# Start of a seven-product MLP kernel: two w1 blocks per load between the first x blocks, half-column products, and 16-bit turns for the later half of x

## The chip, the cores and the metric

The kernel runs on one core of a Trainium2 chip. The metric is the device time of one execution in microseconds (us). All runs told of here are in the fast state: their granted TensorE clock, the mean over an execution, is 0.989 or more of full speed. PE is the TensorE's matmul unit, DVE the VectorE, ACT the ScalarE, POOL the GpSimd, SP the SyncE, which here only issues DMAs.

## The reference

```python
# x[16,256,512], w1[512,4096], w2[2048,512], all float32
h = x @ w1
gate, value = np.split(h, 2, axis=-1)
h = np.maximum(gate, 0) * value
return (h @ w2).astype(np.float32)
```

## The kernel before

The 4096 rows of x are worked off in four stages of 1024 rows. A stage has a first matmul (16 blocks of w1 columns) and a second one (with w2), and the second one of a stage is interleaved with the first blocks of the next stage. Both matmuls are done with seven products in place of eight, on operands in 16 bit. For that, four sums of parts of x (S1 to S4) and four of parts of w1 (T1 to T4) are needed. In stage 0, DVE makes the former once and POOL the latter for two blocks at a time:

```python
def sums_of(o, eng=nc.vector):                     # L164
    for n, i0, i1, op in (("S1", "A21", "A22", ADD), ("S2", "S1", "A11", SUB), ("S4", "A12", "S2", SUB),
                          ("S3", "A11", "A21", SUB)):
        yield eng.tensor_tensor(o[n], o[i0], o[i1], op=op)

def w1_ops(jb, n, t):                              # L215 to L218, two blocks at a time
    ...
    nc.gpsimd.tensor_tensor(op["T1"], b12, b11, op=SUB)
    nc.gpsimd.tensor_tensor(op["T2"], b22, (op["T1"]), op=SUB)
    nc.gpsimd.tensor_tensor(op["T3"], b22, b12, op=SUB)
    nc.gpsimd.tensor_tensor(op["T4"], b21, (op["T2"]), op=SUB)
```

A block's seven products write three PSUM tiles X, Y, W. ACT copies X into Y after P1, and P6, P7 and P4 add to that copy. `P5` needs S1 and T1, `P3` needs S4, `P7` needs S3, and P4 waits until DVE has read Y for `cc` (L266):

```python
WX = {"P1": ("B11", "A11"), "P2": ("B21", "A12"), "P3": ("B22", "S4"), "P4": ("T4", "A22"),
      "P5": ("T1", "S1"), "P6": ("T2", "S2"), "P7": ("T3", "S3")}
def P1(self):
    ...
    self.mm("P1", self.X, True)
    self.Y = psy.tile([P, TH], F32, name="Y", tag="Y")
    nc.scalar.copy(out=self.Y, in_=self.X)         # L240
```

At the very start, x arrives as eight float32 blocks of 128 rows. PE turns (transposes) each of them into PSUM, and DVE and ACT copy one half each into the 16-bit tiles. Since the sums aren't ready then, the first two blocks of w1 are "plain": eight ordinary products. `keep_busy` puts filler products between the turns:

```python
def turn_first(o, h, b, ps):
    for e in range(4):
        nc.tensor.transpose(ps[:, e * P:(e + 1) * P], xn[h][b][:, e * P:(e + 1) * P], ident)
    for k, copy in ((0, nc.vector.tensor_copy), (1, nc.scalar.copy)):
        copy(out=o[f"A{h + 1}{k + 1}"][:, :, b * P:(b + 1) * P], in_=ps[:, k * 256:k * 256 + 256]...)
...
    turn_first(xo, 0, 2, new_x()); keep_busy(2)        # shortened
    turn_first(xo, 0, 3, new_w()); keep_busy(2)
    plain[0].products(0, *first_half, half)            # the first useful products
    ...
    next(sums)                                         # S1
    plain[0].products(1, *second_half, half)
    next(sums); next(sums)                             # S2, S4
    plain[0].products(1, *second_half, other)
    plain[0].value(); plain[0].gate(1)
    prepare(3)
    plain[1].products(1, *second_half)                 # the last plain products; S3 comes in block 2
```

For the later stages, GpSimd casts x to 16 bit from DRAM to DRAM (a casting load) and SP loads it back with eight transposing loads. DVE's four sums for stage 1 stand, in its order of work, ahead of the two evictions L352 and L357 of stage 0's last output pair.

## Time and profile before

| | before |
|---|---|
| median of three runs (lowest to highest) | 313.85 us (313.25 to 314.24) |
| span of the profiled execution | 311.5 us |
| PE busy | 97% |
| first plain product starts | 8.48 us |
| block 2 (first with seven products) starts | 17.19 us |
| block 4 starts | 23.54 us |

The page's lines of busy time and of the chain of waits that ended last, before:

```profile
PE 302.7 (97%) x1870; PEld 182.8 (59%) x1870; DVE 231.2 (74%) x378; ACT 177.9 (57%) x350; POOL 153.9 (49%) x186
...
PE 69%; ACT 2%; issue 0%
```

PE is the limit. There is little to gain but at the start and in single waits. PE's timeline shows those. A line of a timeline has the start in us, the busy time in us, engine, source line, operation, output and inputs, the shape, the number of instructions, and in brackets how long the engine was idle before and what ended that. PE, before:

```profile
8.26 0.38 PE L150 MATMUL Y<-warm 128*128 128x256 f16 x2
8.48 0.38 PE L288 MATMUL X<-x_A_149,w_B_87 128*128 128x256 f16 x2
...
17.19 0.59 PE L233 MATMUL X<-x_A_149,w_B_87 128*128 128x512 f16 x2
17.62 0.59 PE L233 MATMUL W<-x_S_152,w_T_90 128*128 128x512 f16 x2
18.45 0.59 PE L233 MATMUL X<-x_A_150,w_B_88 128*128 128x512 f16 x2 [0.23 <-ACT Y L240]
...
23.11 0.59 PE L233 MATMUL Y<-x_A_151,w_T_93 128*128 128x512 f16 x2 [0.48 <-DVE cc L266]
23.54 0.59 PE L233 MATMUL X<-x_A_149,w_B_87 128*128 128x512 f16 x2
...
85.27 0.59 PE L233 MATMUL W<-x_S_684,w_T_90 128*128 128x512 f16 x2
86.44 0.60 PE L320 MATMUL Y<-v_T_100,g 128*128 128x256 f16 x4 [0.57 <-DVE o L357]
```

A product of two 512-column matmuls takes 0.43 us from start to start (17.19 to 17.62), one of two 256-column matmuls 0.22. The busy column is longer since successive matmuls overlap, so delays below are counted from start to start: 18.45 − 17.62 − 0.43 = 0.40 us lost for the copy of X into Y. From 8.48 to 17.19 no time is lost. The wait at 86.44 loses 0.74 us (85.27 + 0.43 = 85.70).

DVE and POOL, before, in the same view:

```profile
14.93 0.68 DVE L164 TENSOR_TENSOR x_S_152<-x_S_154,x_A_151 128x1024 f16<-128x1024 f16 x1
15.64 1.65 DVE L164 TENSOR_TENSOR x_S_153<-x_S_152,x_A_149 128x1024 f16<-128x1024 f16 x1
17.33 1.53 DVE L164 TENSOR_TENSOR x_S_155<-x_A_150,x_S_153 128x1024 f16<-128x1024 f16 x1
...
82.98 0.69 DVE L164 TENSOR_TENSOR x_S_684<-x_S_686,x_A_683 128x1024 f16<-128x1024 f16 x1 [2.14 <-DMA x_A_683<-x_598]
...
85.97 0.42 DVE L357 SCALAR_TENSOR_TENSOR o<-Y,pu_1002 128x256 f32<-128x256 f32 x1
```

```profile
15.34 1.40 POOL L215 TENSOR_TENSOR w_T_90<-w_stage 128x512 f16<-128x512 f32 x1 [5.42 <-DMA w_stage<-in_w_dram]
16.82 1.48 POOL L216 TENSOR_TENSOR w_T_91<-w_stage,w_T_90 128x512 f16<-128x512 f32 x1
```

The same sum takes 0.68 us alone (14.93, and 82.98) and 1.65 us beside POOL. S1 begins at 14.93, just before POOL's first subtraction at 15.34, and so is still cheap.

### The profile page before, as it was taken

To read this page: it belongs to the slowest core of one execution; us is meant where nothing else is said; L and a number is where in the kernel's file an instruction comes from. 1 tells how busy PE (TensorE), PEld (TensorE's weight loads), DVE (VectorE), ACT (ScalarE), POOL (GpSimd) and SP (SyncE) were. 2 spreads that over 40 slices of the span, in tenths; PEclk is the share of its full clock that TensorE was granted. 3 is DMA by queue.
4 is the path that set the end of the run, shared out by engine and by line. 5 is a ranking of instruction groups with operands and counts; after the bars stand their busy time and mean duration, and the time that the engine had idled before them with its cause. 6 is when DMAs were issued, how large, how long until landed. Compare 5 with 4: busy or idle time off the path is not lost.

```text
span 311.5 us, 5217 instructions
## 1 busy us (share of the span) xinstructions
PE 302.7 (97%) x1870; PEld 182.8 (59%) x1870; DVE 231.2 (74%) x378; ACT 177.9 (57%) x350; POOL 153.9 (49%) x186
## 2 busy tenths in 40 slices
PE   7999999999999999999999999999999999999993
PEld 3934444588844444478864444458884444448883
DVE  1598888889758888887527888888536888888841
ACT  2688885445855555537675555545776555553230
POOL 2199999920058999400028889700007998700000
PEclk9999999999999999999999999999999999999999
DMA  7978695999784233000355400000335110000132
GB/s 241 354 221 258 183 222 76 202 205 151 214 243 102 70 69 67 2 0 36 136 171 117 117 1 3 0 0 9 128 107 164 37 34 1 0 3 0 69 140 66
DMA packets 37340, 32.87 MB, mean 106 GB/s; under 512 B 14400, under 2 KB 32320, under 8 KB 37184
## 3 DMA queue, kind: packets, MB, share of 16 engines
q1 hardware_dynamic: 31904, 25.70, 27.5%
q0 software_dynamic: 4352, 6.29, 11.8%
q10 hardware_dynamic: 1056, 0.52, 0.6%
q8 instruction: 15, 0.25, 0.3%
q14 instruction: 13, 0.11, 0.1%
HBM read 27.26 MB, written 12.58 MB: 128 GB/s over the span
## 4 chain that ended last, share of the span: by engine, by line
PE 69%; ACT 2%; issue 0%
PE Y L233 20%; PE X L233 13%; PE W L233 13%; PE Y L320 10%; PE X L320 7%; PE W L320 6%; ACT sq L179 1%; ACT Y L240 0%; ACT o L363 0%; ACT pu_1812 L347 0%; PE X L527 0%; ACT pu_2615 L347 0%
## 5 line engine op out<-in xcount | busy, mean ns | idle before, releaser
L170 POOL TENSOR_TENSOR fold<-xh 128x1024 f32<-128x1024 f16 x16 | 30.3, 1895 | 95.0 <-DMA xh<-x_696 35.0
L260 DVE SCALAR_TENSOR_TENSOR cc<-W,pu 128x512 f32<-128x512 f32 x62 | 42.9, 692 | 33.7 <-ACT pu L254 30.5
L254 ACT ACTIVATE pu<-Y 128x512 f32<-128x512 f32 x62 | 37.1, 598 | 34.9 <-PE Y L233 33.7
L240 ACT COPY Y<-X 128x512 f32<-128x512 f32 x62 | 35.4, 571 | 37.3 <-PE X L233 21.2
L173 POOL TENSOR_TENSOR fold<-fold 128x512 f32<-128x512 f32 (+2 forms) x96 | 51.9, 540 | 7.5
L320 PEld LDWEIGHTS <-w_stage 128*128 128x128 f16 x512 | 50.0, 98 | 5.9
L261 DVE SCALAR_TENSOR_TENSOR g<-X,cc 128x512 f16<-128x512 f32 x62 | 42.9, 692 | 2.3
L270 DVE SCALAR_TENSOR_TENSOR g<-Y,cc 128x512 f16<-128x512 f32 x62 | 42.3, 682 | 2.8 <-PE Y L233 2.8
L320 PEld LDWEIGHTS <-g 128*128 128x128 f16 x384 | 37.5, 98 | 9.0 <-issue 0.9
L266 DVE SCALAR_TENSOR_TENSOR cc<-Y,pu 128x512 f32<-128x512 f32 x62 | 42.3, 682 | 0.2
L247 ACT ACTIVATE pu<-W 128x512 f32<-128x512 f32 x62 | 37.1, 599 | 0.0
L164 DVE TENSOR_TENSOR w_stage<-g 128x1024 f16<-128x1024 f16 x32 | 21.4, 686 | 0.2
L233 PEld LDWEIGHTS <-w_T_93 128*128 128x128 f16 x124 | 12.0, 97 | 16.0 <-issue 4.2
L233 PEld LDWEIGHTS <-w_B_88 128*128 128x128 f16 x124 | 12.1, 98 | 15.0 <-issue 1.1
L233 PEld LDWEIGHTS <-w_B_89 128*128 128x128 f16 x124 | 12.1, 98 | 14.8 <-issue 0.3
L233 PEld LDWEIGHTS <-w_T_90 128*128 128x128 f16 x124 | 12.1, 98 | 14.7
L233 PEld LDWEIGHTS <-w_T_91 128*128 128x128 f16 x124 | 12.1, 98 | 14.7
L233 PEld LDWEIGHTS <-w_T_92 128*128 128x128 f16 x124 | 12.1, 98 | 13.8 <-issue 0.2
L233 PEld LDWEIGHTS <-w_B_87 128*128 128x128 f16 x124 | 11.9, 96 | 13.5
L320 PE MATMUL Y<-v_T_100,g 128*128 128x256 f16 x128 | 17.1, 273 | 0.6 <-DVE o L357 0.6
L320 PE MATMUL Y<-v_T_98,w_stage 128*128 128x256 f16 x128 | 16.8, 273 | 0.0
L320 PE MATMUL W<-v_B_96,w_stage 128*128 128x256 f16 x128 | 16.6, 273 | 0.0
(218 smaller groups left out, 565.4 us busy)
## 6 DMA issues: line engine op xcount, KB each, us to landing
out_dram<-o SPq DMA_DIRECT2D x30, 256.0 KB, 2.0
w_stage<-in_w_dram SPq DMA_DIRECT2D x14, 512.0 KB, 5.5
x_598<-in_x_dram POOLq DMA_DIRECT2D x1, 1024.0 KB, 10.1
x_653<-in_x_dram POOLq DMA_DIRECT2D x1, 1024.0 KB, 16.0
x_696<-in_x_dram POOLq DMA_DIRECT2D x1, 1024.0 KB, 19.8
xh<-x_653 SPq DMA_DIRECT2D x4, 256.0 KB, 3.4
xh<-x_598 SPq DMA_DIRECT2D x4, 256.0 KB, 3.9
x_1346<-in_x_dram POOLq DMA_DIRECT2D x1, 1024.0 KB, 7.5
```

Of the source, the lines that this page charges most:

```text
L164: yield eng.tensor_tensor(o[n], o[i0], o[i1], op=op)
L170: nc.gpsimd.tensor_tensor(fold, t, t, op=MULT)
L173: nc.gpsimd.tensor_tensor(fold[:, :, :m], fold[:, :, :m], fold[:, :, m:2 * m], op=ADD)
L233: nc.tensor.matmul(ps, wop[wn][:, b, self.jb * P:(self.jb + 1) * P], self.xo[xn][:, b, :], start=fresh and b == 0, stop=b == 1, skip_group ...
L240: nc.scalar.copy(out=self.Y, in_=self.X)
L247: nc.scalar.activation(self.p5, self.W, COPY, scale=GS)
L254: nc.scalar.activation(self.u2, self.Y, COPY, scale=GS)
L260: nc.vector.scalar_tensor_tensor(out=self.c12, in0=self.W, scalar=GS, in1=self.u2, op0=MULT, op1=ADD)
L261: nc.vector.scalar_tensor_tensor(out=self.g[:, self.jb, :TH], in0=self.X, scalar=0.0, in1=self.c12, op0=MAX, op1=MULT)
L266: nc.vector.scalar_tensor_tensor(out=self.c22, in0=self.Y, scalar=GS, in1=self.p5, op0=MULT, op1=ADD)
L270: nc.vector.scalar_tensor_tensor(out=self.g[:, self.jb, TH:], in0=self.Y, scalar=0.0, in1=self.c22, op0=MAX, op1=MULT)
L320: nc.tensor.matmul(ps, self.op[an][:, i], vop[wn][:, i], start=name in ("P1", "P5") and i == 0, stop=i == NJ // 2 - 1, skip_group_check=True)
```

## The change

The intent is an earlier and denser start. The first two w1 blocks come in one load (rows of 1 KB in place of 512 B), its gate half ahead of x1 and its value half between x1 and x2, so that gate products of half the columns can begin with two x blocks. The later half of x is cast to 16 bit and turned at 16 bit. In the program, the three sums S1, S2, S4 stand ahead of the last plain products, and one last group of plain products moves behind block 2's second product, where it covers the copy of X into Y. The diff, cut to its core:

```diff
-    wl = [(0, 1, 0), (1, 1, 1)] + [(jb, 2, jb % 6) for jb in range(2, NJ, 2)]
+    wl = [(jb, 2, jb % 6) for jb in range(0, NJ, 2)]
 ... (plain_w: DVE and ACT cast these w1 blocks; POOL did most of it before)
-    fetch(0, nc.scalar)
-    fetch_first(0)
-    fetch(1, nc.sync)
+    fetch_first(0, 0)
+    fetch(0, nc.scalar, (0,))
+    fetch_first(0, 1)
+    fetch(0, nc.sync, (1,))
+    fetch_first(0, 2, 3)
+    fetch_first(1, 0, 1, 2, 3)
 ... (turn_first: 16-bit rows and a 16-bit identity for the later half)
+    ys = [new_y(), new_y()]
+    turn_first(xo, 0, 0, *ys)
+    keep_busy(6)
+    turn_first(xo, 0, 1, new_x(), new_x())
+    for y in ys:
+        nc.tensor.matmul(y, warm_b[:, :P], warm_b[:, :TH], start=True, stop=True)
+    for p in plain:
+        p.open()
+        p.part("gate", *first_half, half)
+    turns = new_x()
+    turn_first(xo, 0, 2, turns[:, :2 * P], turns[:, 2 * P:])
+    for p in plain:
+        p.part("value", *first_half, half)
+    turn_first(xo, 0, 3, turns[:, :2 * P], turns[:, 2 * P:])
+    cast_first(0, nc.gpsimd.tensor_copy)
+    cast_first(1, nc.vector.tensor_copy)
+    cast_first(2, nc.gpsimd.tensor_copy)
 ... (16-bit turns between the other plain products, in the banks turns and turns2)
-    next(sums)
-    plain[0].products(1, *second_half, half)
+    plain[1].products(*second_half, half)
     next(sums)
     next(sums)
-    plain[0].products(1, *second_half, other)
+    next(sums)
+    plain[0].products(*second_half, other)
     plain[0].value()
     plain[0].gate(1)
-    plain[1].products(1, *second_half)
+    def last_plain():
+        plain[1].products(*second_half, other)
+        plain[1].value()
+        next(sums)
+        plain[1].gate(1)
 ...
                 if s == 0 and (n, jb) == ("P5", NPLAIN):
-                    next(sums)
-                    plain[1].gate(1)
+                    last_plain()
```

More of the change, by code (lines that the diff above doesn't have):

```diff
@@ L142, in fast_way @@
     ident = wpool.tile([P, P], F32, name="ident")
+    Y = psy.tile([P, TH], F32, name="Y", tag="Y")
     for i in range(NWARM):
-        Y = psy.tile([P, TH], F32, name="Y", tag="Y")
         nc.tensor.matmul(Y, warm_b[:, :P], warm_b[:, :TH], start=True, stop=True)
@@ L201, in load_rows, with load_w1 @@
         return t
-    def load_w1(eng, jb, n, u):
+    def load_w1(eng, jb, n, u, halves=(0, 1)):
         t = w_stage[:, u:u + n].rearrange("p u v -> p (u v)").rearrange("p (g e j) -> p g e j", g=2, e=4)
-        for v in range(2):
+        for v in halves:
             eng.dma_start(out=t[:, v], in_=w1_v[v, :, :, jb * P:(jb + n) * P])
@@ L277, in __init__, with open, part, products @@
             self.g, self.jb = g, jb
-        def products(self, h, a1, a2, cols=(0, TH)):
+        def open(self):
+            self.X = psx.tile([P, TH], F32, name="X", tag="X")
+            self.W = psw.tile([P, TH], F32, name="W", tag="W")
+        def part(self, which, a1, a2, cols):
             js, c = slice(self.jb * P, (self.jb + 1) * P), slice(*cols)
-            if cols[0] == 0:
-                self.X = psx.tile([P, TH], F32, name="X", tag="X")
-                self.W = psw.tile([P, TH], F32, name="W", tag="W")
-            for a, gate, value in ((a1, "B11", "T3"), (a2, "B21", "B22")):
-                for ps, wn in ((self.X, gate), (self.W, value)):
-                    for b in range(2):
-                        nc.tensor.matmul(ps[:, c], wop[wn][:, b, js], a[:, b, c], start=a is a1 and b == 0,
-                                         stop=a is a2 and b == 1)
+            ps, names = (self.X, ("B11", "B21")) if which == "gate" else (self.W, ("T3", "B22"))
+            for a, wn in zip((a1, a2), names):
+                for b in range(2):
+                    nc.tensor.matmul(ps[:, c], wop[wn][:, b, js], a[:, b, c], start=a is a1 and b == 0,
+                                     stop=a is a2 and b == 1)
+        def products(self, a1, a2, cols):
+            if cols[0] == 0:
+                self.open()
+            self.part("gate", a1, a2, cols)
+            self.part("value", a1, a2, cols)
         def value(self):
@@ L389, in advance, with fetch @@
             next(stream, 0)
-    wl = [(0, 1, 0), (1, 1, 1)] + [(jb, 2, jb % 6) for jb in range(2, NJ, 2)]
+    wl = [(jb, 2, jb % 6) for jb in range(0, NJ, 2)]
     ws, copies = {}, []
-    def fetch(i, eng):
+    def fetch(i, eng, halves=(0, 1)):
         if i < len(wl):
@@ L398, in fetch @@
             jb, n, u = wl[i]
-            ws[i] = load_w1(eng, jb, n, u)
+            ws[i] = load_w1(eng, jb, n, u, halves)
     def prepare(i):
@@ L408, in copy_some, with plain_w @@
         del copies[:n]
-    def plain_w(i):
-        jb, n, _ = wl[i]
-        t = ws.pop(i)
+    def plain_w(v):
+        jb, n, _ = wl[0]
         js = slice(jb * P, (jb + n) * P)
-        for n, k, v in (("B11", 0, 0), ("B21", 1, 0), ("T3", 0, 1)):
-            nc.gpsimd.tensor_copy(out=wop[n][:, :, js], in_=t[:, k, :, v])
-        return lambda: nc.scalar.copy(out=wop["B22"][:, :, js], in_=t[:, 1, :, 1])
+        for (wn, k), copy in zip(((("B11", 0), ("B21", 1)), (("T3", 0), ("B22", 1)))[v], (nc.vector.tensor_copy, nc.scalar.copy)):
+            copy(out=wop[wn][:, :, js], in_=ws[0][:, k, :, v])
     def plain_w_end(jb, n, i):
@@ L427, in fast_way, with fetch_first, cast_first, turn_first @@
     xn = [[t.rearrange("p a b -> p (a b)").bitcast(F32) for t in place[4 * h:4 * h + 4]] for h in range(2)]
-    def fetch_first(h):
-        for b in range(4):
+    x16_first = [halfs.tile([P, 8, P], F16, name="xh", tag="xh").rearrange("p (b q) c -> p b (q c)", b=2) for _ in range(2)]
+    ident16 = wpool.tile([P, P], F16, name="ident16")
+    def fetch_first(h, *bs):
+        for b in bs:
             nc.sync.dma_start(out=xn[h][b], in_=x_nat[0, h, b])
-    def turn_first(o, h, b, ps):
+    def cast_first(b, copy):
+        copy(out=x16_first[b // 2][:, b % 2], in_=xn[1][b])
+    def turn_first(o, h, b, *ps):
+        rows, one = (x16_first[b // 2][:, b % 2], ident16) if h else (xn[0][b], ident)
         for e in range(4):
-            nc.tensor.transpose(ps[:, e * P:(e + 1) * P], xn[h][b][:, e * P:(e + 1) * P], ident)
+            nc.tensor.transpose(ps[e // 2][:, e % 2 * P:(e % 2 + 1) * P], rows[:, e * P:(e + 1) * P], one)
         for k, copy in ((0, nc.vector.tensor_copy), (1, nc.scalar.copy)):
             copy(out=o[f"A{h + 1}{k + 1}"][:, :, b * P:(b + 1) * P],
-                 in_=ps[:, k * 256:k * 256 + 256].rearrange("p (b t) -> p b t", b=2))
+                 in_=ps[k][:, :2 * P].rearrange("p (b t) -> p b t", b=2))
     def new_x():
         return psx.tile([P, TH], F32, name="X", tag="X")
+    def new_y():
+        return psy.tile([P, TH], F32, name="Y", tag="Y")
     def new_w():
         return psw.tile([P, TH], F32, name="W", tag="W")
-    fetch(0, nc.scalar)
-    fetch_first(0)
+    fetch_first(0, 0)
+    fetch(0, nc.scalar, (0,))
+    fetch_first(0, 1)
+    fetch(0, nc.sync, (1,))
+    make_identity(nc, ident)
+    fetch_first(0, 2, 3)
+    fetch_first(1, 0, 1, 2, 3)
     fetch(1, nc.sync)
-    make_identity(nc, ident)
-    fetch_first(1)
     fetch(2, nc.sync)
-    fetch(3, nc.sync)
+    nc.vector.tensor_copy(out=ident16, in_=ident)
     xo = x_tiles()
@@ L456, in fast_way @@
     half, other = (0, TH // 2), (TH // 2, TH)
-    rest = plain_w(0)
-    turn_first(xo, 0, 0, new_w())
-    keep_busy(2)
-    turn_first(xo, 0, 1, new_x())
-    rest()
-    keep_busy(4)
-    turn_first(xo, 0, 2, new_x())
-    keep_busy(2)
-    turn_first(xo, 0, 3, new_w())
-    keep_busy(2)
-    plain[0].products(0, *first_half, half)
-    plain_w(1)()
-    fetch(4, nc.sync)
-    plain[0].products(0, *first_half, other)
-    plain[0].value()
-    plain[0].gate(0)
-    plain[1].products(0, *first_half, half)
@@ L474, in fast_way @@
-    ps = [new_x(), new_w()]
-    for b in range(4):
-        turn_first(xo, 1, b, ps[b % 2])
-        if b == 1:
-            plain[1].products(0, *first_half, other)
-            plain[1].value()
-    plain[1].gate(0)
-    sums = sums_of(xo)
-    prepare(2)
-    copy_some(3)
-    fetch(5, nc.sync)
-    next(sums)
-    plain[0].products(1, *second_half, half)
+    ys = [new_y(), new_y()]
+    turn_first(xo, 0, 0, *ys)
+    keep_busy(6)
+    plain_w(0)
+    turn_first(xo, 0, 1, new_x(), new_x())
@@ new lines, in fast_way @@
+    for y in ys:
[3 more added lines that the diff above has]
+        p.part("gate", *first_half, half)
+    plain_w(1)
+    turns = new_x()
[6 more added lines that the diff above has]
+    cast_first(2, nc.gpsimd.tensor_copy)
@@ new lines, in fast_way @@
+    fetch(3, nc.sync)
+    plain[0].products(*first_half, other)
+    plain[0].value()
+    turns = turns.bitcast(F16)
+    turn_first(xo, 1, 0, turns[:, :2 * P], turns[:, 2 * P:])
+    plain[0].gate(0)
+    plain[1].products(*first_half, other)
+    plain[1].value()
+    turns2 = new_w().bitcast(F16)
+    turn_first(xo, 1, 1, turns2[:, :2 * P], turns2[:, 2 * P:])
+    cast_first(3, nc.vector.tensor_copy)
+    plain[1].gate(0)
+    turn_first(xo, 1, 2, turns[:, :2 * P], turns[:, 2 * P:])
+    plain[0].products(*second_half, half)
@@ L487, in fast_way @@
+    turn_first(xo, 1, 3, turns2[:, :2 * P], turns2[:, 2 * P:])
+    sums = sums_of(xo)
+    prepare(1)
+    copy_some(3)
+    fetch(4, nc.sync)
+    plain[1].products(*second_half, half)
     next(sums)
     next(sums)
-    plain[0].products(1, *second_half, other)
+    next(sums)
+    plain[0].products(*second_half, other)
     plain[0].value()
     plain[0].gate(1)
-    prepare(3)
-    plain[1].products(1, *second_half)
+    prepare(2)
+    def last_plain():
+        plain[1].products(*second_half, other)
+        plain[1].value()
+        next(sums)
+        plain[1].gate(1)
@@ L551, in fast_way @@
         last = NJ * PERIOD
-        todo = 3
+        todo = 2
         for at in range(first * PERIOD, (NJ - 1) * PERIOD + 14):
@@ L562, in fast_way @@
                         prepare(todo)
-                    if 5 <= todo < 9:
-                        n2 = ("B11", "T3", "B22", "B21")[todo - 5]
-                        nc.gpsimd.dma_start(out=vop[n2], in_=w2_v[(0, 0, 1, 1)[todo - 5], (0, 1, 1, 0)[todo - 5]])
+                    if 4 <= todo < 8:
+                        n2 = ("B11", "T3", "B22", "B21")[todo - 4]
+                        nc.gpsimd.dma_start(out=vop[n2], in_=w2_v[(0, 0, 1, 1)[todo - 4], (0, 1, 1, 0)[todo - 4]])
                 if (s, n, jb) == (0, "P7", 13):
@@ L581, in fast_way @@
                 getattr(blocks[jb], n)()
-                if s == 0 and (n, jb) == ("P1", NPLAIN):
-                    plain[1].value()
                 if s == 0 and (n, jb) == ("P5", NPLAIN):
-                    next(sums)
-                    plain[1].gate(1)
+                    last_plain()
                 if n in ("P6", "P7"):
@@ L589, in fast_way @@
                 if s == 0 and n == "P7" and jb % 2:
-                    fetch(jb // 2 + 5, nc.sync)
+                    fetch(jb // 2 + 4, nc.sync)
                 if n == "P6" and (s, jb) in LOOKX:
```

## The prediction

> **What bounds the kernel now.** The TensorE: the page has it busy 302.7 of 311.5 us (97%); the table by stretches shows over 99% from 60 to 300 us. The change touches only the start. In the timeline of before, PE warms up to 4.40, turns x with fillers to 8.48, then works without a gap to 18.05, and then has gaps of 0.40 us (copy of X into Y), 0.14 us, and 0.64 us (block 2's last product waits for the DVE's cc). Block 4 starts at 23.54. Fillers and waits from 4.4 to 8.48 cost 2.3 us, the gaps 1.2 us: 3.5 us are all there is to win.
>
> **What the change does, costed.**
> - Removes: half of the cost of turning the last four x blocks. A float32 turn takes 0.43 us of PE; I estimate 0.22 at 16 bits, so -0.87 us. The Trainium skill, "TensorE: Matmul & The Clock Gate" (Part 4), says a turned block lands in PSUM and needs a copy; the trace agrees (0.42 us DVE, 0.37 us ACT), and that part does not shrink.
> - Moves: w1's halves go between x blocks, so I estimate x2 at 8.1 us instead of 7.0, x3 at 8.9 instead of 7.75. Gate halves of both blocks fill the time: the first product starts near 7.1 us instead of 8.48.
> - Adds on DVE: two w1 casts and two x casts, estimated 0.35 to 0.5 us each from the 0.42 us of a 128x256 PSUM copy: 1.8 us. Before, POOL cast w1. POOL gets two x casts.
> - Moves one half-column group (0.87 us of PE) behind block 2's second product, where it covers the wait for the Y copy.
>
> **How much is on the critical path.** After x2 lands comes a serial line: turn 0.43, value products 0.87, turn 0.43, DVE copy 0.45, ACT copy of the same bank 0.4 (before, ACT starts there after DVE), products; so x4's copy starts on DVE near 11.6. From there DVE owes x copies, casts, two gates and four sums. The sums run slowly while POOL makes T1 to T4 (1.65, 1.53, 1.16 us against 0.69 for the same shape later); the last gate should end near 22 us against 21.14. So S4 (third product of block 2), S3 (its P7) and cc become PE waits, estimated 3 us together. Blocks 2 and 3 of w1 should land 0.5 us earlier (POOL starts at 14.8 instead of 15.34), which helps little. Sum: about -1.6 us from early start and cheaper turns, -1.0 from covered gaps, +3.0 of new waits: a small loss, +0.4 us, with wide doubt, since the intent was a gain and x2 may land earlier.
>
> **Predicted time:** 314.3 us, 8 in 10 between 312.6 and 315.7. Faster by over 2%: 1%. Within 2%: 98.5%. Slower by over 2%: 0.5%.
>
> **What would show each step.** First product near 7.1 us; x2 turned near 8.1; PE idle 0.5 to 0.8 us after x3's turn; 16-bit turns at 0.22 us; no gap after the copy of X into Y; PE waits for DVE sums at P3 and P7 of block 2; block 4's first product at 23.9 (before 23.54), and from there the same distance to the end.
>
> **What would make it wrong.** If x2 lands before 7.6 us, or DVE casts from SBUF cost under 0.3 us, or the sums don't suffer from POOL, DVE is not late and the change gains about 1 us. If PE's clock falls back during early waits, it loses more.

## The result, and the profile after

| | before | after |
|---|---|---|
| median of four runs (lowest to highest) | 313.83 us (313.25 to 314.24) | 315.15 us (315.03 to 315.67) |
| ratio (95% interval) | 1 | 1.0043 (1.0027 to 1.0059) |
| span of the profiled execution | 311.5 us | 313.2 us |

A ratio is the mean time of one kernel's fast runs over that of the other's of the same rounds, so not quite the ratio of the medians. The change loses 1.3 us: within 2%, but a loss that the interval resolves. The result is correct.

The page's lines of busy time and of the chain of waits, after:

```profile
PE 303.4 (97%) x1876; PEld 182.4 (58%) x1876; DVE 233.6 (75%) x383; ACT 178.4 (57%) x350; POOL 153.2 (49%) x182
...
PE 88%; DVE 5%; ACT 2%; DMA 2%; issue 1%; SPq 0%; DVEq 0%
```

PE works 0.7 us more. The two lines of shares can't be compared: before, the view follows the chain back only to 86.40 us (its shares sum to 71%), and now it reaches back to the load of an x block. So DVE's 5% and the DMA's 2% are the start coming into view, and are no measure of what the change added. Its pieces from 8 to 26 us, cut (start us, us, what), after:

```profile
2.27 6.07 DMA x_A<-in_x_dram
...
9.14 0.44 DVE x_A L452
...
9.60 0.38 ACT x_A L452
...
10.02 0.67 PE X L450 x4
...
10.79 0.44 DVE x_A L452
...
16.47 1.49 DVE x_S L164
...
17.98 1.65 DVE x_S L164
```

PE, after, in the timeline:

```profile
7.16 1.03 PE L289 MATMUL X<-x_A,w_B 128*128 128x256 f16 x8
8.47 0.63 PE L450 MATMUL X<-ident,x_A 128*128 128x128 f32 x4 [0.28 <-DMA x_A<-in_x_dram]
...
10.02 0.66 PE L450 MATMUL X<-ident,x_S 128*128 128x128 f32 x4
11.27 0.78 PE L289 MATMUL X<-x_A,w_B 128*128 128x256 f16 x4 [0.59 <-DVE x_A L452]
...
12.33 0.39 PE L450 MATMUL X<-ident,xh 128*128 128x128 f16 x4
12.55 0.60 PE L289 MATMUL X<-x_A,w_B 128*128 128x256 f16 x4
...
16.49 0.38 PE L289 MATMUL W<-x_S,w_T 128*128 128x256 f16 x2 [0.42 <-ACT x_A L452]
...
17.79 0.59 PE L233 MATMUL X<-x_A,w_B 128*128 128x512 f16 x2
18.64 0.59 PE L233 MATMUL W<-x_S,w_T 128*128 128x512 f16 x2 [0.25 <-ACT v L301]
...
21.25 0.60 PE L233 MATMUL W<-x_S,w_B 128*128 128x512 f16 x2 [0.28 <-DVE x_S L164]
...
23.02 0.59 PE L233 MATMUL Y<-x_S,w_T 128*128 128x512 f16 x2 [0.15 <-DVE x_S L164]
...
25.45 0.59 PE L233 MATMUL Y<-x_A,w_T 128*128 128x512 f16 x2 [0.54 <-DVE cc L266]
25.88 0.59 PE L233 MATMUL X<-x_A,w_B 128*128 128x512 f16 x2
...
87.58 0.59 PE L233 MATMUL W<-x_S,w_T 128*128 128x512 f16 x2
88.01 0.60 PE L329 MATMUL Y<-v_T,g 128*128 128x256 f16 x4
```

Compare it with the lines of before mark by mark:

| us from the start | before | after | after − before |
|---|---|---|---|
| first plain product | 8.48 | 7.16 | −1.32 |
| block 2's first product | 17.19 | 17.79, with 0.87 us of plain products still owed | +1.47 |
| block 4's first product | 23.54 | 25.88 | +2.34 |
| stage 0's second matmul | 60.37 | 62.66 | +2.29 |
| the product behind the wait at 86 us | 86.44 | 88.01 | +1.57 |
| stage 1's second matmul | 134.22 | 135.78 | +1.56 |
| last group of products | 305.64 | 307.38 | +1.74 |

**The plain products lose 2.79 us** (first to second mark). Before, 8.71 us without a gap. After, 0.87 us of it is put off, the turns of x2 and x3 (0.87 us, earlier ahead of the first product) fall inside, and four 16-bit turns at 0.22 us instead of 0.43 us save 0.87: 7.84 us of work in 10.63 us. So the waits are 10.63 − 7.84 = 2.79 us. They are 0.44 for x2's load (8.47 instead of 7.16 + 0.87 = 8.03), then 0.21, 0.82 and 0.18 from x3's turn and its copies, 0.51 in two pieces at 14.19 and 14.60, and 0.58 at 16.49, where the bank that a turn used is not copied out. (These pieces sum to 2.74, the rest is rounding.) The reason for the middle ones is in the chain's pieces: x2's and x3's turns share one PSUM bank, so DVE copies (9.14), then ACT (9.60), then PE turns (10.02), then DVE copies again. The Trainium skill, "PSUM — Partial Sum Buffer", section "PSUM bank collisions raise a hardware error", says that two engines may not touch one bank (in the same partitions) at once and that software must put them in order. The trace agrees as far as it goes: with both halves of x2 in one bank, ACT's copy starts at 9.60, just after the end of DVE's, which began at 9.14 and took 0.42.

**Blocks 2 and 3 lose 0.87 us more** (8.09 − 0.87 owed = 7.22 against 6.35). The waits there were 1.17 us before and are 2.04 after: the gap after the copy into Y is gone as intended, but PE now waits for a value of the plain blocks (18.64), for the sums S4 (21.25) and S3 (23.02) and for cc (25.45). DVE and POOL, after, show why:

```profile
16.47 3.15 DVE L164 TENSOR_TENSOR x_S<-x_S,x_A 128x1024 f16<-128x1024 f16 x2 [0.44 <-ACT x_A L452]
19.66 1.53 DVE L164 TENSOR_TENSOR x_S<-x_A,x_S 128x1024 f16<-128x1024 f16 x1
...
21.71 1.16 DVE L164 TENSOR_TENSOR x_S<-x_A,x_S 128x1024 f16<-128x1024 f16 x1
...
83.26 1.42 DVE L164 TENSOR_TENSOR x_S<-x_S,x_A 128x1024 f16<-128x1024 f16 x2
```

```profile
14.89 1.27 POOL L215 TENSOR_TENSOR w_T<-w_stage 128x512 f16<-128x512 f32 x1 [3.18 <-DMA w_stage<-in_w_dram]
16.25 1.16 POOL L216 TENSOR_TENSOR w_T<-w_stage,w_T 128x512 f16<-128x512 f32 x1
17.36 1.72 POOL L217 TENSOR_TENSOR w_T<-w_stage 128x512 f16<-128x512 f32 x1
19.03 1.61 POOL L218 TENSOR_TENSOR w_T<-w_stage,w_T 128x512 f16<-128x512 f32 x1
```

The sums start at 16.47 instead of 14.93, and POOL's subtractions at 14.89 instead of 15.34. So S1, which got ahead of POOL before and took 0.68 us, now takes 1.49 (the chain shows the pair's two parts). The numbers have a strict pattern. Each slow sum ends 0.55 us after the end of the subtraction in the course of which it began: S1 at 17.96 (T2 ends at 17.41), S2 at 19.63 (T3 ends at 19.08), S4 at 21.19 (T4 ends at 20.64). Before, S2 ends at 17.29, and T1 at 16.74. That is a queue, not a slowdown by some share. The Trainium skill, "SBUF — State Buffer", section "SBUF: two separate sides", calls the port pair that the two engines share "an exclusive lock", taken by a DVE operation with two SBUF inputs against a GpSimd operation that reads SBUF: the later one waits out the earlier. This trace agrees but for 0.14 us: alone a sum takes 0.69 us, and here it ends 0.55 us after the subtraction.

**At 86 us, 0.74 us comes back.** In the kernel before PE waits there; after, the product at 88.01 follows its predecessor by 0.43 us, without a wait. DVE's sums for stage 1 begin just after the last transposing load has landed (they start at 82.98 and 83.26), at nearly the same time in both, and the eviction L357, which PE's product needs, stands behind them. The kernel before gets there early and waits. The change gets there 2.3 us later, and the sums are over.

### The profile page after: what moved, and what is told of

It is laid out like the page before. It is cut to its first block, busy times and chain, and to the rows that moved or that the text cites. A ratio compares the mean times of both kernels' runs of the same rounds, so it can differ in the third digit from the quotient of the medians.

```text
span 313.2 us, 5226 instructions
## 1 busy us (share of the span) xinstructions
PE 303.4 (97%) x1876; PEld 182.4 (58%) x1876; DVE 233.6 (75%) x383; ACT 178.4 (57%) x350; POOL 153.2 (49%) x182
## 4 chain that ended last, share of the span: by engine, by line
PE 88%; DVE 5%; ACT 2%; DMA 2%; issue 1%; SPq 0%; DVEq 0%
PE Y L233 25%; PE X L233 16%; PE W L233 16%; PE Y L329 13%; PE X L329 9%; PE W L329 8%; DMA x_A<-in_x_dram 2%; DVE x_S L164 2%; ACT sq L179 1%; DVE g L261 1%; DVE cc L260 1%; DVE g L304 1%; DVE cc L266 1%; PE X L289 0%; PE X L450 0%
## 5 line engine op out<-in xcount | busy, mean ns | idle before, releaser
L233 PEld LDWEIGHTS <-w_T 128*128 128x128 f16 x496 | 48.3, 97 | 60.1 <-issue 3.4
L233 PE MATMUL X<-x_A,w_B 128*128 128x512 f16 x248 | 73.7, 378 | 0.3
L233 PE MATMUL Y<-x_S,w_T 128*128 128x512 f16 x248 | 73.8, 379 | 0.2 <-DVE x_S L164 0.2
L233 PEld LDWEIGHTS <-w_B 128*128 128x128 f16 x372 | 36.1, 97 | 43.0 <-issue 0.9
L233 PE MATMUL Y<-x_A,w_T 128*128 128x512 f16 x124 | 36.7, 377 | 0.8 <-DVE cc L266 0.7
L233 PE MATMUL W<-x_S,w_B 128*128 128x512 f16 x124 | 36.9, 379 | 0.3 <-DVE x_S L164 0.3
L233 PE MATMUL W<-x_S,w_T 128*128 128x512 f16 x124 | 36.9, 379 | 0.3 <-ACT v L301 0.3
L329 PE MATMUL Y<-v_T,w_stage 128*128 128x256 f16 x256 | 33.2, 273 | 0.0
L329 PE MATMUL X<-v_B,g 128*128 128x256 f16 x256 | 31.9, 273 | 0.0
L361 DVE SCALAR_TENSOR_TENSOR o<-W,pu 128x256 f32<-128x256 f32 x16 | 6.8, 423 | 18.9 <-PE W L329 11.8
```

Of the source, the lines that this page charges most:

```text
L233: nc.tensor.matmul(ps, wop[wn][:, b, self.jb * P:(self.jb + 1) * P], self.xo[xn][:, b, :], start=fresh and b == 0, stop=b == 1, skip_group ...
L329: nc.tensor.matmul(ps, self.op[an][:, i], vop[wn][:, i], start=name in ("P1", "P5") and i == 0, stop=i == NJ // 2 - 1, skip_group_check=True)
```

## The experiments

Labels with a_ are edits of the kernel after, those with b_ of the kernel before. The experiments ran in four batches, each beside runs of the kernel before, whose medians were 313.34, 313.28, 313.34 and 313.59 us. Ratios are against the kernel before.

The first theory (A) was that x2's late load and the shared PSUM banks hold up the turned blocks, and that late sums follow from that. Its main rival (B) was that the DVE has too much to do with the added casts. Later rounds tested POOL's part in the sums and the parts of the change alone.

| run | ratio (95%) | median us | block 4 | stage 0, second matmul | stage 1, second matmul |
|---|---|---|---|---|---|
| before | 1 | | 23.54 | 60.37 | 134.22 |
| the change | 1.0043 (1.0027 to 1.0059) | 315.15 | 25.88 | 62.66 | 135.78 |
| a_banks | 1.0026 (1.0005 to 1.0047) | 314.06 | 24.68 | 61.26 | 134.38 |
| a_x_before_values | 1.0017 (0.9998 to 1.0036) | 313.93 | 24.54 | 61.12 | 134.23 |
| a_pool_casts | 1.0042 (1.0024 to 1.0060) | 314.78 | 25.88 | 62.38 | 135.50 |
| a_last_inline | 1.0060 (1.0042 to 1.0078) | 315.30 | 25.88 | 62.66 | 135.80 |
| a_pool_quiet | 1.0024 (1.0000 to 1.0047) | 314.24 | 24.80 | 61.62 | 134.75 |
| b_turns_16 | 0.9997 (0.9977 to 1.0018) | 313.30 | 22.44 | 58.94 | 134.03 |
| b_last_later | 1.0017 (0.9999 to 1.0036) | 313.94 | 23.57 | 60.07 | 134.18 |
| b_turns_16_last_later | 0.9992 (0.9970 to 1.0013) | 313.13 | 22.66 | 59.48 | 134.28 |
| b_casts_later | 1.0169 (1.0146 to 1.0193) | 318.54 | 23.68 | 60.49 | 139.27 |
| b_turns_16_casts_later | 1.0166 (1.0133 to 1.0198) | 318.00 | 22.52 | 59.01 | 139.09 |
| a_casts_later | 1.0156 (1.0123 to 1.0189) | 318.24 | 25.98 | 62.74 | 137.36 |
| b_turns_16_one_cast_later | 1.0124 (1.0101 to 1.0147) | 317.14 | 22.56 | 59.06 | 137.84 |

The three right columns are us from the start of the profiled execution. Many of the timed differences are at the edge of what the rounds resolve, so the marks in the trace decide. Each mark comes from one execution. Where kernels differ only after block 4, that mark repeats within 0.14 us (23.54 and 23.68; 25.88 and 25.98; 22.44, 22.52 and 22.56), so smaller differences at block 4 mean nothing.

### a_banks: each half of a turned block in a bank of its own

```diff
-    turns = new_x()
-    turn_first(xo, 0, 2, turns[:, :2 * P], turns[:, 2 * P:])
+    turn_first(xo, 0, 2, new_y(), new_y())
 ... (x3 the same way; x4 to x7 with new_y().bitcast(F16))
```

> The changed kernel, but every turned x block from x2 on goes to two PSUM banks of the Y pool, so that the DVE copy and the ScalarE copy of a block run side by side and no product waits for a bank. Theory A (the serial line from x2's landing through turn, copies, turn, copies to the DVE sums is the critical chain): x3's second copy no longer waits for its first (0.45 us), the 0.58 us PE wait before 16.5 us goes, the sums start about 0.7 to 1.0 us earlier, block 4 starts at about 25.0 instead of 25.88 us, ratio to before about 1.001 to 1.002. Rival B (the DVE is simply overloaded by the casts): sums start at most 0.3 us earlier, ratio stays 1.004.

Block 2's first product came at 16.50 (the change: 17.79), the first sum at 15.36 (16.47), block 4 at 24.68 (25.88): the shared banks cost 1.2 of the 2.34 us. In a second point the kernel failed: its result is wrong, which was not intended (relative error 0.254). I use its marks all the same: from block 4 to stage 0's second matmul this run takes 36.58 us and the change 36.78, so the wrong values slowed nothing that shows. The cause of the error was argued and not tested: the Trainium skill, "PSUM — Partial Sum Buffer", section "The four PSUM rules", says that PSUM keeps status bits that decide whether a matmul adds or overwrites, that an ACT write leaves them as they are, and that a group's first matmul and any transpose of 2-byte elements clear those of their bank. P6 adds to ACT's copy in Y, so it would overwrite the copy after 16-bit turns in that bank. It would also explain why the change runs two 512-column products into `ys` after turning x0 there, which fills only half of each bank.

### a_x_before_values: also x2 and x3 loaded ahead of w1's value half

```diff
+    fetch_first(0, 2, 3)
     fetch(0, nc.sync, (1,))
-    fetch_first(0, 2, 3)
 ... (gate products of both halves of the columns first, values after; turns as in a_banks)
```

> As a_banks, and x2 and x3 are loaded ahead of w1's value half, with all gate products before any value product. Theory A: x2 lands near 7.1 us instead of 8.34, first-half work ends about 1 us earlier than in a_banks, the sums start 1.5 to 2 us earlier than in the changed kernel, block 4 starts near 24.0 us, ratio 0.998 to 1.000. Rival B: gain below 0.3 us over a_banks, since DVE's casts stay.

The result is wrong by the same error. Block 4 came at 24.54, only 0.14 us ahead of a_banks, which is within the noise. In this run x0's turn took 1.09 us (0.75 in a_banks) and the six fillers 1.24 (0.82), for no reason that the trace shows, and the first product started at 7.72 (7.30). x2 did land earlier, and its turn waited for no load. But counted from the first product, block 2 came after 9.46 us here and after 9.20 in a_banks, so the new order of loads brought no gain up to there. Theory A had block 4 near 24.0: that part of it missed.

### a_pool_casts: DVE's two x casts given to GpSimd

```diff
-    cast_first(1, nc.vector.tensor_copy)
+    cast_first(1, nc.gpsimd.tensor_copy)
 ... (block 3 the same way)
```

> The changed kernel with the two DVE casts of x blocks (0.86 and 0.42 us in its trace) on GpSimd, 0.62 us each, where it is idle. Rival B (DVE overloaded): sums start about 0.7 us or more earlier, block 4 near 25.0, ratio near 1.002. Theory A: DVE had idle time around both casts, sums start 0.1 to 0.4 us earlier, ratio 1.003 to 1.004.

The result is correct. With DVE relieved, the sums start at 16.50 (the change: 16.47) and block 4 at 25.88, the same. DVE's x casts do not hold anything up. Nor can its two w1 casts (5.67 and 7.68 us): after them DVE is idle for 1.03 us before its next copy at 9.14. Theory B fell.

### a_last_inline: the last plain products back ahead of block 2

```diff
-    def last_plain():
-        plain[1].products(*second_half, other)
-        plain[1].value()
-        next(sums)
-        plain[1].gate(1)
+    plain[1].products(*second_half, other)
 ... (its value and gate around block 2's P1 and P5, as in the kernel before)
```

> The changed kernel with the last four plain products back in front of block 2 and the order of the sums as before (one part undone). If deferring them helps as intended: the copy of X into Y is again followed by a PE gap of 0.3 to 0.4 us and the ratio rises to about 1.005 or 1.006. If the deferral itself caused the loss (third sum and gates later on DVE): the ratio falls to about 1.002.

The result is correct. The gap after the copy into Y is back (0.23 us idle at 19.93), and the wait for S4 after it is 0.30 us, ending at 21.25 as in the change. Block 4 starts at 25.88 in both. DVE's chain of sums and cc sets that mark, so moving the products neither helped nor hurt. The timed ratios' intervals overlap.

### a_pool_quiet: blocks 2 and 3 without POOL's subtractions

```diff
-        nc.gpsimd.tensor_tensor(op["T1"], b12, b11, op=SUB)
+        if jb != NPLAIN:
+            nc.gpsimd.tensor_tensor(op["T1"], b12, b11, op=SUB)
 ... (T2 to T4 the same way; a memset of these columns early on stands in for them)
```

> Wrong result on purpose: the changed kernel with T1 to T4 of blocks 2 and 3 set to zero by GpSimd at the start, so that GpSimd does nothing while the first sums run. If GpSimd's work slows the DVE sums (1.49, 1.65, 1.53 us): the first sums take about 0.69 us each until blocks 4 and 5 are prepared, S4 ends about 2 us earlier, the PE waits for S4, S3 and cc shrink, and block 4 starts at about 24.4 instead of 25.88 us. If the sums are slow for another reason, their times stay and block 4 stays within 0.3 us.

DVE in this run, the sums:

```profile
16.89 1.42 DVE L164 TENSOR_TENSOR x_S<-x_S,x_A 128x1024 f16<-128x1024 f16 x2 [0.44 <-ACT x_A L453]
18.34 1.64 DVE L164 TENSOR_TENSOR x_S<-x_A,x_S 128x1024 f16<-128x1024 f16 x1
```

S1 and S2 took 1.42 us together in place of 3.15. POOL resumed at 17.92 with the next pair of blocks, and S4, begun after that, took 1.64 again. Blocks 2 and 3 took 6.58 us from the first product to block 4 (the change: 8.09), so POOL's subtractions cost 1.5 us there, and with the sums earlier PE has no wait for S4, S3 or cc left. This run's block 2 started 0.43 us late (18.22), so block 4 at 24.80 understates it. The 1.2 us of a_banks and these 1.5 us are more than the 2.34 us that block 4 is behind, so their gains can't simply be added; each accounts for about half or more, and the two were not tried together.

This run shows one thing more. With four subtractions fewer, GpSimd issued its casting loads of x earlier (the first at 51.71 us instead of 54.17 in the change), and the last of the transposing loads behind them landed at 79.31 instead of 83.14. So the moment at 83 us, at which the sums for stage 1 can begin, hangs on GpSimd's own work in stage 0.

### b_turns_16: 16-bit turns alone, in the kernel before

```diff
+        rows, one = ...             # shortened: 16-bit rows and identity for the later half
+        if h:
+            ps = ps.bitcast(F16)
         for e in range(4):
-            nc.tensor.transpose(ps[:, e * P:(e + 1) * P], xn[h][b][:, e * P:(e + 1) * P], ident)
+            nc.tensor.transpose(ps[:, e * P:(e + 1) * P], rows[:, e * P:(e + 1) * P], one)
 ... (four casts on GpSimd, a 16-bit identity)
```

> The kernel before, with only the 16-bit turning of the later half of x added, all four casts on the idle GpSimd. If 16-bit turning is a gain by itself: PE does the four turns in 0.22 instead of 0.43 us each, the first sum starts near 14.2 instead of 14.93 us, block 4 starts near 22.9 instead of 23.54, ratio about 0.998. If DVE and GpSimd are the limit anyway: block 4 within 0.2 us, ratio 1.000.

The result is correct. This part of the change does what it should: block 4 starts at 22.44, 1.10 us ahead of before, since S1 and S2 now come ahead of POOL as a pair (1.41 us). The lead is 1.43 us at 58.94. Then it is gone. PE in this run:

```profile
83.93 0.59 PE L233 MATMUL W<-x_S,w_T 128*128 128x512 f16 x2
86.02 0.60 PE L320 MATMUL Y<-v_T,g 128*128 128x256 f16 x4 [1.49 <-DVE o L357]
```

The loss at this point is 86.02 − 83.93 − 0.43 = 1.66 us, where it was 0.74 before and is 0 in the change. DVE's sums wait until 82.56 for a transposing load, and that moment hardly moves. Stage 1's second matmul starts 0.19 us ahead of before, and the time is the same (0.9997).

### b_last_later: the deferral alone, in the kernel before

```diff
     next(sums)
     next(sums)
+    plain[1].products(1, *second_half, half)
 ...
-    plain[1].products(1, *second_half)
+    def last_plain(): ...       # as in the change, called after block 2's P5
```

> The kernel before, with only the deferral of the last plain products behind block 2's second product, and three sums ahead of the gates. If the deferral covers the wait for the copy of X into Y: the 0.40 us gap at 18.05 goes, block 4 starts near 23.1 to 23.3, ratio 0.998 to 0.999. If it only moves the wait to the DVE sums: block 4 near 23.5, ratio 1.000.

The result is correct. The gap after the copy into Y is gone, but P5 waits 0.25 us for ACT's value and P4 still waits 0.40 us for cc. DVE's sums keep their order and their times (S1 at 14.96). Block 4 starts at 23.57 against 23.54: the wait is only moved.

### b_turns_16_last_later: both parts

Its edit is that of b_turns_16 with that of b_last_later.

> Both parts on the kernel before, without its new order of loads. If the loss of the changed kernel comes from its load order and the serial line behind x2: this one beats both, block 4 near 22.4 us. Part of that lead may be lost at 86 us, where the kernel before waits 0.57 us for sums of the next x, whose load hangs on GpSimd's chain: ratio 0.995 to 0.998. If the parts don't add: ratio 0.999 to 1.000.

The result is correct. Block 4 starts at 22.66, P5 of block 2 now waits 0.31 us for POOL's T1, the wait at 86 us is 1.5 us, and the ratio of 0.9992 (0.9970 to 1.0013) is no resolved gain.

### b_casts_later, b_turns_16_casts_later, a_casts_later: casting loads held back

These were to move the transposing loads, and with them DVE's sums at 83 us, forward: two of GpSimd's casting loads wait until they have landed.

```diff
-    CASTS = {(0, 11): 1, (0, 13): 0, (0, 14): 2, (1, 8): 3}
+    CASTS = {(0, 11): 1, (1, 8): 3}
 ... (tick: a small tile for the waiting copy)
+    def cast_after(s, t, k):
+        nc.gpsimd.tensor_copy(out=tick[:, k:k + 1], in_=t[:, 1, TH - 1:TH])
+        cast_x(s)
 ...
+                if (s, n, jb) == (0, "P1", NJ - 1):
+                    cast_after(0, xo_next["A12"], 0)
+                    cast_after(2, xo_next["A22"], 1)
```

> The kernel before with only the two casting loads of x for the third and the first stage held until the transposing loads of the second x have landed (a one-column GpSimd copy waits for them). If the 0.57 us PE wait at 86 us comes from those loads running beside the transposes: the transposes land several us earlier (first sum of the next x before 80 instead of 82.98 us), the wait is gone, ratio about 0.998. If the transposes are slow on their own: no change, ratio 1.000.

> The kernel before with 16-bit turning and the same holding back. If the lead of 1.1 us of 16-bit turning at block 4 was eaten only by the wait at 86 us (1.5 us there): the wait goes and the kernel keeps the lead, ratio 0.994 to 0.996. If another appointment eats it: 0.998 or more.

> The changed kernel with the same holding back. It has no wait at 86 us, since it comes there 2.3 us late; if that wait is why the loss is 1.7 us and not 2.3 us, the holding back gains it nothing: ratio stays near 1.0043, and the changed kernel stands about 0.7% behind the kernel before with the same holding back. If it gains as much as the kernel before does, the explanation is wrong.

All three results are correct, and all three are slower by some 1.6%. Their executions scatter by up to 3.3 us (a_casts_later: 316.51 to 319.83), so one profile shows one case of several. In b_casts_later the first four transposing loads took 5.51 us to issue, against 11.0 before, but the last one still landed at about 82.4. The wait at 86 us went to nearly nothing in b_casts_later, and was 1.9 us in b_turns_16_casts_later. A new one came: PE idle 3.7 us to 94.10 in b_casts_later, 3.2 us in b_turns_16_casts_later, 1.1 us in a_casts_later. After 3.7 us idle, b_casts_later's products follow each other at 0.81 to 0.85 us instead of 0.43 until 97.43, and the granted clock from 95 to 97 us is 0.50. The Trainium skill, "TensorE: Matmul & The Clock Gate", Part 1, says the clock falls to half after an idle window of about 3.4 us; here it did after waits of 3.2 and 3.7 us, the first a little under the page's figure, and not after the 1.1 us of a_casts_later (0.43 us again from its second product on). The expectations missed, and these runs don't answer what a free DVE at 83 us would be worth.

### b_turns_16_one_cast_later: only one casting load held back

```diff
-    CASTS = {(0, 11): 1, (0, 13): 0, (0, 14): 2, (1, 8): 3}
+    CASTS = {(0, 11): 1, (0, 13): 0, (1, 8): 3}
 ... (with the edit of b_turns_16)
+                if (s, n, jb) == (0, "P1", NJ - 1):
+                    cast_after(2, xo_next["A22"], 1)
```

> The kernel before with 16-bit turning, and only the casting load for the third stage held until the second x has been transposed; the one for the first stage stays where it was, since its later use made SyncE and the PE wait at 94 us in the last three runs. If the wait at 86 us is what eats the lead of 16-bit turning: the last transposes land near 78 us instead of 82.6, the wait goes, nothing waits at 94 us, ratio 0.994 to 0.997. If the transposes don't land earlier: wait and ratio (0.9997) as without the holding back. If the third stage's x comes too late now: a new wait after 150 us and a ratio over 1.000.

The result is correct. DVE's sums, which wait for the transposing loads, began at 81.55 instead of 82.56. PE in this run, and then ACT:

```profile
85.02 0.60 PE L320 MATMUL Y<-v_T,g 128*128 128x256 f16 x4 [0.45 <-DVE o L357]
...
92.69 1.01 PE L233 MATMUL W<-x_S,w_B 128*128 128x512 f16 x2 [3.19 <-ACT pu L247]
```

```profile
92.05 0.60 ACT L247 ACTIVATE pu<-W 128x512 f32<-128x512 f32 x1 [3.66 <-DMA out_dram<-o]
```

The wait for L357 fell from 1.49 to 0.45 us: when those loads land earlier, the wait shrinks, as the reading of 86 us says. But ACT waited 3.66 us for an output store to free its buffer, and PE 3.19 us for ACT. The trace has the held casting load in flight there (issued at 81.64, landed 9.8 us later). Beside it the longest output store of this stretch took 9.7 us from issue to landing, where the longest of the same stretch before took 3.2, and SP needed from 85.09 to 91.71 to issue three row loads of x, for which it needed 1.44 us before. So the gain can't be collected this way. Whether an order of DVE with the two evictions ahead of the four sums would collect it was not tried and stays open, and so does lighter work for GpSimd ahead of its casting loads (see a_pool_quiet). So does what a_banks and a_pool_quiet would give with correct data. No kernel tried is clearly faster than the one before.

## Why the prediction was right or wrong

The prediction was right: 315.15 us lies in its range of 312.6 to 315.7, and a small loss within 2% was the likeliest class. That the number fits is partly luck, though: block 4 came about 2 us later than predicted (25.88, not 23.9), and 0.74 us of the loss then came back at 86 us, where the prediction had not looked. Without that the median would have been near 315.9 us (an estimate, 315.15 + 0.74), outside the range.

- **The start.** "The first product starts near 7.1 us" measured 7.16. x2 landed at 8.34 and was turned at 8.47 (predicted 8.1). The 16-bit turn took 0.22 us (12.33 to 12.55), as estimated, and the copy did not vanish. DVE's copy did shrink, though, from 0.42 to 0.29 us, where the prediction said that part would not; ACT's stayed at 0.37.
- **The serial line** was the right mechanism, but mis-sized. PE's idle time after x3's turn was 0.59 us (predicted 0.5 to 0.8). But x4's copy came at 12.82, not 11.6, and the waits for copies at 14.19, 14.60 and 16.49 (1.09 us) were not foreseen. a_banks shows that the shared banks cost 1.2 us at block 4.
- **DVE late, and sums beside POOL.** Right as a mechanism: PE waits at P3, P7 and cc, no gap after the copy into Y, POOL at 14.89 (predicted 14.8). Not in the sum was that S1 would also fall into POOL's time (1.49 us, not 0.68). So the last plain gate ended at 23.48, not near 22. a_pool_quiet bears out only a part of the condition that the prediction named, "the sums don't suffer from POOL": with POOL quiet, 1.5 us come back, but the predicted gain of about 1 us does not come (block 4 at 24.80, still behind 23.54). The other one, DVE's casts, was of no account (a_pool_casts).
- **The mis-sized term** is "+3.0 of new waits". Counted from start to start, the waits after are 2.79 + 2.04 = 4.83 us. The early start gave 1.32 us, as the cheaper 16-bit turns only paid for the two float turns that moved inside (predicted 1.6). So block 4 is at 1.32 earlier, 4.83 of waits and 1.17 of old waits removed: +2.34, where +0.4 was predicted.
- **The wrong step** is "from there the same distance to the end". The kernel before loses 0.74 us at 86 us, and a later kernel does not: +2.29 became +1.57. b_turns_16 shows the same from the other side: of 1.43 us of lead, 0.92 went at that point. With +1.74 at the last group of products, and +1.3 in the medians, the result landed inside the range. The gap between these last two, one profiled execution and a median of runs, is within the interval of the ratio (313.83 us times 0.0027 to 0.0059, so 0.8 to 1.9 us).

## What to carry to other kernels

An earlier start is worth only what the slowest chain behind it lets through, so follow each early piece of work until the first wait that does not depend on it; here that was a load landing at 83 us, which hung on GpSimd and not on PE. When two engines queue for one port, ask which of them comes first in the new order, not only how slow each is beside the other: being 0.4 us ahead of POOL was worth 0.8 us for the first sum. And before two transfers are moved apart, look at what else will stand in the queue beside the one that was moved.

## What the Trainium skill lacked or had wrong

- "TensorE: Matmul & The Clock Gate", Part 4, gives about 275 ns in a kernel for the transpose of a 128x128 block at 16 bit and says that a transpose does not bring the full clock about. Here four of them took 0.22 us from start to start, so 0.055 us each, as fast as the products around them stream (0.22 us for the same 512 columns). So the page's figure is the duration of one and not what each of a run of them costs; a longer run of turns alone was not tried.
- "SBUF — State Buffer", "SBUF: two separate sides", has the exclusive lock between DVE and GpSimd right, and no time for a DVE sum behind a GpSimd subtraction. Here a 16-bit sum of 128x1024 took 0.69 us alone and, begun inside a GpSimd subtraction, ended 0.54 to 0.58 us after it in every such instance of these runs (it then took 0.69 to 1.65 us in all).
- No page that I read gives a figure for what a GpSimd casting load from DRAM to DRAM does to loads issued beside it. Four transposing loads took 11.0 us to issue beside two casting loads and 5.5 us without; three row loads took 1.44 us without and 6.4 to 6.6 us beside one in three runs.
